# A hybrid RG-LRU and attention layer on one core: scores in one run, the gate row inside w_o, a regrouped last stage

## The chip, the cores and the metric

The kernel runs on one core of one Trainium2 chip. The metric is device time in microseconds (us); three runs of the kernel before have a median of 577.61 us (577.07 to 577.84). Engines: TensorE (PE) multiplies matrices into PSUM, which has eight banks of 128x512 float32; VectorE (DVE), ScalarE (ACT) and GpSimd (POOL) work element by element; SyncE (SP) issues the loads and stores.

## The reference

One encoder layer on x of 512 tokens by 1024 channels, in float32. With h = rms_norm(x) * (1 + scl) + shift (shift, scl and a gate row come from c), one product h @ w_in gives eight parts of 1024 columns: xa, za, q, k, v, zb, ga, gb. Then two branches are merged:

```
xa  = conv4(xa); per direction: r, i = sigmoid(block_diag(xa)); a = exp(-8 r softplus(-lam))
h   = scan of a*h + sqrt(1 - a^2) * (i*xa), forward and backward
y_a = ((h_fwd + h_bwd) * silu(za)) @ w_pa
y_b = (neighbourhood_attention(q, k, v, rpb) * silu(zb)) @ w_pb     # 16 heads of 64, window 8 x 16
merged = sigmoid(ga) * y_a + sigmoid(gb) * y_b
out = rms_norm(x + gate * (merged @ w_o), g_final)
```

The gate is a row of 1024 numbers, one for each column of the output, so it multiplies the product merged @ w_o column by column.

## The kernel before

**Precision and shapes.** Every product of two float32 matrices is done as three TensorE matmuls on a high and a low part (helper mm3, recorded at line 342): high by high, high by low, low by high. The high part is a cast on ScalarE (line 336), the low part a subtraction on VectorE or GpSimd (line 339). Channels lie on the 128 partitions and the 512 tokens along the free axis, so a projection tile of 128 columns of w_in is 8 x 3 = 24 matmuls of 128x512 into one PSUM bank (class acc).

**Stages.** First the norm, h and v; then for each of eight head pairs the projections of q, k and z with the attention of the pair between them; then four groups of two channel tiles of the recurrent branch (projections, gates, scan) with y_b @ w_pb; then ga, y_a @ w_pa and the merge; at the end the output product.

**What sets the order.** The operations are not issued as they are written. Each is given to a planner (class Plan) with an engine, a cost, a rank, and the tiles that it reads and writes; the planner runs a list schedule and fixes one order per engine. It also hands out the slots of SBUF and the eight banks of PSUM. LIMITS says how many banks a class may hold: acc 3, sp (scores) 2, pt (transposes) 2, pv (products with v) 2, mi 2, gt (gates) 4.

**Attention of a pair** (function attention, line 682). The 512 queries are four blocks of 128; two heads lie on partitions 0 to 63 and 64 to 127. half(b0) does two blocks: scores issues 12 matmuls with 64 rows, 192 or 256 columns, into two sp banks (one per head); VectorE adds the bias and takes the minimum (line 718); ScalarE takes the exponential (724); TensorE transposes (733, tile pt); ScalarE and VectorE split the transposed block (738, 740, tile pp); TensorE multiplies with v (tile pv); ScalarE and VectorE add the parts (755, 758, 761, tiles vp and yt). After both halves come the reciprocals (tile rcx, transposed at line 781 into mi) and the product with silu(zb).

**Gates** (conv_gates, line 851). For each channel tile and each direction d, 6 matmuls with 64 rows write two gt banks, which ScalarE reads with four tanh.

**The gate row and w_o.** gate_row (line 968) builds the row, broadcast to 128 partitions, in two halves of 512 columns (tiles gate) with half the value, and g_final likewise (gfin). w_o is loaded in eight blocks of 128 rows (tile wo), cast (woh) and split (wol) from line 1033 on. The output product goes tile by tile of 128 tokens; mhl is the merged tile. Its first 512 columns (o0) are followed by the other 512 (o1), those of the last tile in two pieces of 256.

**The epilogue** (epi, line 1049) for each piece: multiply by gate (1055), add x (1057), squares and their sum on ScalarE (1065; on VectorE, line 1061, for the last piece), multiply by g_final (1067), and once a tile is whole, the root and its refinement (rstd_ops, lines 409 to 418), the scaling, and stores from SyncE (1084, 1087, 1090).

Of the kernel before, what the change touches and what calls it, by code (L numbers as in the profile page):

```python
# [13 lines left out]
P = 128  # L14
S = 512
D = 1024
# [15 lines left out]
LIMITS = {"hx": 8, "acc": 3, "sp": 2, "pt": 2, "pv": 2, "mi": 2, "gt": 4}  # L32
# [261 lines left out]
def layer(ctx, tc, x, par, w_m, w_g, bc_gate, w_v, w_in, w_blk, rpb, amask, w_pa, w_pb, w_o, g_final, out):  # L294
# [387 lines left out]
    def attention(pr, q, k, z, nbt, pos):  # L682
# [10 lines left out]
        off = (pr % 2) * 256  # L693
        def half(b0):
            sp = [B("sp"), B("sp")]
            spv = lambda h, e: sp[h].ap.rearrange("p (e f) -> p e f", e=2)[:, e, :]
            rk = pos + 0.1 * b0
            nks = [ROWS * BLOCKS[b0 + e][1] for e in range(2)]

            def scores(e_):  # L700
                for e in range(2):
                    kc0, w, _ = BLOCKS[b0 + e]
                    for i, (qt, kt) in enumerate(((qh, kh), (qh, kl), (ql, kh))):
                        for h in range(2):
                            kv = kt.ap.rearrange("p (r c) -> p r c", c=GW)[H[h], :, kc0:kc0 + w]
                            mm(spv(h, e)[:, :nks[e]], qt.ap[H[h], (b0 + e) * P:(b0 + e + 1) * P], kv, i == 0, i == 2)
            op("PE", 0.85, scores, rk, r=[qh, ql, kh, kl], w=sp, name=f"qk{pr}")
# [143 lines left out]
    def conv_gates(i, xa):  # L851
# [16 lines left out]
        for d in range(2):  # L868
            bk = [B("gt"), B("gt")]

            def f(e_, d=d, bk=bk):
                for m, (w, xx) in enumerate(((g[0], xh), (g[0], xl), (g[1], xh))):
                    for e in range(2):
                        mm(bk[e].ap, w.ap[H[e], c0 + d * P:c0 + (d + 1) * P], xx.ap[H[e], :], m == 0, m == 2)
# [12 lines left out]
            op("DVE", dve(512), lambda e, u=u: nc.vector.scalar_tensor_tensor(u.ap, u.ap, 1.0, xc.ap, op0=ALU.add, op1=ALU.mult),  # L887
               n + 0.6, r=[xc], rw=[u], lock=True, name="ix")
# [160 lines left out]
    def epi(t, c0, w, o, rank, last):  # L1049
# [5 lines left out]
        op("DVE", dve(w), lambda e: nc.vector.tensor_tensor(y(), o.ap[:, :w], gate[n].ap[:, gs], op=ALU.mult), rank,  # L1055
           r=[o, gate[n]], w=[yo[t]], name="e0")
        op("DVE", dve(w), lambda e: nc.vector.tensor_tensor(y(), y(), xr(), op=ALU.add), rank, r=[xres[t, n]], rw=[yo[t]],  # L1057
           lock=True, name="e1")
# [5 lines left out]
        else:  # L1064
            op("ACT", act(w, 0, True), lambda e: nc.scalar.activation(xr(), y(), AF.Square, accum_out=ssq.ap), rank,  # L1065
               r=[yo[t]], w=[ssq, xres[t, n]])
            op(("DVE", "POOL"), (dve(w), pool_(w)), lambda e: ENGINE[e].tensor_tensor(y(), y(), gfin[n].ap[:, gs], op=ALU.mult),  # L1067
               rank + 0.1, r=[gfin[n]], rw=[yo[t]], lock=True, name="e2")
        if not last:
            if t in ssum:  # L1070
                a = ssum[t]
                op("DVE", 0.16, lambda e: nc.vector.tensor_tensor(a.ap, a.ap, ssq.ap, op=ALU.add), rank + 0.1, r=[ssq], rw=[a])
            else:
                ssum[t] = ssq
            return
        rs, a = C("rs", 1, 6), ssum[t]
        rstd_ops(1, [a, ssq], lambda: (a.ap, ssq.ap), rank, rs)
        if final:
            op("DVE", dve(w), lambda e: nc.vector.scalar_tensor_tensor(y(), y(), rs.ap, gfin[n].ap[:, gs], op0=ALU.mult, op1=ALU.mult),
               rank, r=[rs, gfin[n]], rw=[yo[t]], lock=True)  # L1080
            z = lambda: yo[t].ap[:, 512:c0]
            op("DVE", dve2(w), lambda e: nc.vector.tensor_scalar(z(), z(), rs.ap, None, op0=ALU.mult), rank, r=[rs], rw=[yo[t]],
               lock=True)
            op("SP", 0.45, lambda e: nc.sync.dma_start(out[rows, 512:], yo[t].ap[:, 512:]), rank, r=[yo[t]], size=262144)
            zz = lambda: yo[t].ap[:, :512]
            op("ACT", act(512, 1), lambda e: nc.scalar.activation(zz(), zz(), AF.Copy, scale=rs.ap), rank, r=[rs], rw=[yo[t]])
            op("SP", 0.45, lambda e: nc.sync.dma_start(out[rows, :512], zz()), rank, r=[yo[t]], size=262144)
# [103 lines left out]
```

## Time and profile before

| what | value |
|---|---|
| median of three runs | 577.61 us (577.07 to 577.84) |
| profiled execution: time, span | 577.42 us, 575.70 us |
| mean granted TensorE clock | 0.997 |
| busy: PE, DVE, ACT, POOL | 98%, 70%, 59%, 16% |
| chain that ended last: PE, DVE | 97%, 1% |

A page lists the busy time of each engine, the span in slices, the chain of work that ended last, and groups of instructions by line. The timeline of a view merges equal instructions that follow each other (x4) and puts idle time ahead of them in brackets with what ended it. Ends of matmuls are modelled, and they overlap: a 128x512 matmul has a modelled length of 390 ns. Starts are what counts there. The time of the execution is 1.72 us longer than the span, which goes from its first to its last instruction.

### The profile page before, as it was taken

The numbers are of one execution on the slowest core, as the hardware profiler recorded it, in microseconds if no ns is written. First come the engines' busy times: TensorE is split into PE (matmuls) and PEld (weight loads), VectorE is DVE, ScalarE is ACT, GpSimd is POOL, SyncE is SP. The second block draws the span as 40 slices with busy tenths as digits, with TensorE's granted clock in tenths as the row PEclk, the third lists the DMA queues.
The fourth block names the chain that finished last, engine by engine and source line by source line (L and its number), as shares of the span: only waits on it lengthen the run. The fifth ranks groups of instructions, "written<-read, shape, count | busy, mean of one in ns | idle before, by whom it ended". The sixth has DMA issues, their size and how long they took to land.

```text
span 575.7 us, 7726 instructions
## 1 busy us (share of the span) xinstructions
PE 566.2 (98%) x2829; PEld 465.1 (81%) x2829; DVE 404.4 (70%) x690; ACT 337.1 (59%) x584; POOL 91.7 (16%) x82
## 2 busy tenths in 40 slices
PE   8999999999999999999999999999999999999994
PEld 6888878888888888887887787788788888888884
DVE  5997966776776867786479649739847996465444
ACT  5864536646546557469948875993994333252132
POOL 0004428264273470000000000000000000000010
PEclk9999999999999999999999999999999999999998
DMA  8993987544435321123232123123239813380002
GB/s 286 409 406 93 351 246 219 189 112 147 115 96 175 83 101 48 63 77 125 73 111 92 68 79 129 45 102 109 74 95 326 273 38 109 123 316 1 0 38 110
DMA packets 30814, 81.34 MB, mean 141 GB/s; under 512 B 3264, under 2 KB 6456, under 8 KB 30777
## 3 DMA queue, kind: packets, MB, share of 16 engines
q1 hardware_dynamic: 30777, 80.86, 42.3%
q8 instruction: 22, 0.36, 0.3%
q14 instruction: 15, 0.12, 0.1%
HBM read 74.56 MB, written 6.29 MB: 140 GB/s over the span
## 4 chain that ended last, share of the span: by engine, by line
PE 97%; DVE 1%; ACT 0%; issue 0%; POOL 0%; POOLq 0%; ACTq 0%
PE acc L342 76%; PE hx L342 8%; PE pv L342 3%; PE pt L733 3%; PE sp L342 2%; PE gt L342 2%; PE mi L457 2%; PE hx L386 1%; PE hx L471 1%; PE mi L781 1%; ACT xr L1065 0%; DVE yo L1057 0%; DVE yo L1055 0%; DVE q L412 0%; PE mi L342 0%
## 5 line engine op out<-in xcount | busy, mean ns | idle before, releaser
L342 PE MATMUL acc<-hhl,whi 128*128 128x512 f32 x784 | 247.8, 398 | 0.0
L342 PEld LDWEIGHTS acc<-hhl,whi 128*128 128x128 f32 x784 | 141.6, 188 | 29.1 <-issue 2.9
L342 PE MATMUL acc<-hhl,wlo 128*128 128x512 f32 x392 | 153.2, 391 | 0.0
L342 PEld LDWEIGHTS acc<-hhl,wlo 128*128 128x128 f32 x392 | 73.7, 188 | 15.9
L336 ACT CAST whi<-wraw 128x1024 fp32r<-128x1024 f32 x72 | 74.2, 1046 | 3.4 <-DMA wraw<-in_w_in_dram 2.6
L339 DVE TENSOR_TENSOR wlo<-wraw,whi 128x1024 fp32r<-128x1024 f32 x49 | 59.2, 1220 | 12.0 <-ACT whi L336 11.1
L339 POOL TENSOR_TENSOR wlo<-wraw,whi 128x1024 fp32r<-128x1024 f32 x23 | 55.2, 2404 | 73.0 <-ACT whi L336 59.5
L1067 POOL TENSOR_TENSOR yo<-yo,gfin 128x512 f32<-128x512 f32 x4 | 5.2, 1288 | 344.0 <-ACT xr L1065 344.0
L724 ACT ACTIVATE p<-p,mn 128x192 f32<-128x192 f32 (+1 forms) x64 | 30.4, 477 | 28.8 <-DVE mn L718 28.8
L342 PE MATMUL acc<-woh,mhl 128*128 128x512 f32 (+1 forms) x144 | 40.4, 366 | 0.0
L947 DVE SCALAR_TENSOR_TENSOR gm<-gm,acc 128x512 f32<-128x512 f32 x16 | 11.0, 688 | 41.7 <-PE acc L342 41.7
L662 POOL TENSOR_TENSOR nb<-msk,braw 128x192 f32<-128x192 f32 (+1 forms) x48 | 31.0, 677 | 56.4 <-DMA braw<-in_rpb_dram 56.4
L342 PE MATMUL acc<-yahl,whi 128*128 128x512 f32 x128 | 39.5, 390 | 0.0
L342 PE MATMUL acc<-ybhl,whi 128*128 128x512 f32 x128 | 39.4, 390 | 0.0
L718 DVE CUSTOM_DVE_ANT_0 p<-sp,nb 128x192 f32<-128x192 f32 (+1 forms) x64 | 32.4, 614 | 7.6 <-PE sp L342 7.2
L342 PE MATMUL hx<-vh,hhl 128*128 128x512 f32 x112 | 35.4, 391 | 0.0
L740 DVE TENSOR_TENSOR pp<-pt,pp 96x512 fp32r<-96x512 f32 (+1 forms) x32 | 22.0, 687 | 11.7 <-ACT pp L738 11.7
L342 PEld LDWEIGHTS acc<-woh,mhl 128*128 128x128 f32 x144 | 26.1, 189 | 4.4
L342 PEld LDWEIGHTS acc<-yahl,whi 128*128 128x128 f32 x128 | 24.0, 188 | 5.0
L342 PEld LDWEIGHTS acc<-ybhl,whi 128*128 128x128 f32 x128 | 24.0, 188 | 5.0
L342 PE MATMUL acc<-wol,mhl 128*128 128x512 f32 (+1 forms) x72 | 26.3, 366 | 0.0
L758 DVE TENSOR_TENSOR vp<-pv,vp 64x256 f32<-64x256 f32 x32 | 13.5, 421 | 18.1 <-ACT vp L755 17.6
(183 smaller groups left out, 1004.6 us busy)
## 6 DMA issues: line engine op xcount, KB each, us to landing
wraw<-in_w_in_dram SPq DMA_DIRECT2D x56, 512.0 KB
wc<-in_w_m_dram SPq DMA_DIRECT2D x16, 512.0 KB
vscr<-va SPq DMA_DIRECT2D x8, 512.0 KB
vt<-vscr SPq DMA_DIRECT2D x16, 256.0 KB
wraw<-in_w_pb_dram SPq DMA_DIRECT2D x8, 512.0 KB
wraw<-in_w_pa_dram SPq DMA_DIRECT2D x8, 512.0 KB
wr<-in_w_g_dram SPq DMA_DIRECT2D x16, 256.0 KB
wo<-in_w_o_dram SPq DMA_DIRECT2D x8, 512.0 KB
```

What stands on the lines that cost most here:

```text
L336: return lambda e: nc.scalar.copy(o(), i()) if e == "ACT" else nc.vector.tensor_copy(o(), i())
L339: return lambda e: ENGINE[e].tensor_tensor(o(), a(), b().bitcast(F32), op=ALU.subtract)
L342: nc.tensor.matmul(o, a, b, start=first, stop=last)
L386: op("PE", 0.9, lambda e, n=n, cb=cb: nc.tensor.matmul(cb.ap, onesc.ap[0:1, :], crow.ap[0:1, n * 512:(n + 1) * 512], start=True, stop=True ...
L457: op("PE", 0.3, lambda e: nc.tensor.matmul(wb.ap[:, :P], onesc.ap, onesc.ap, start=True, stop=True), 5000 + j, r=[onesc], w=[wb], until=un ...
L662: nc.gpsimd.tensor_tensor(o, mv, view, op=ALU.subtract)
L718: nc.vector.tensor_tensor_reduce(out=o, in0=v(spv(h, e)[:, :nk]), in1=v(hv(nb)[:, h, :nk]), scale=1.0, scalar=3e38, op0=ALU.add, op1=ALU.m ...
L724: nc.scalar.activation(hv(pt_)[:, h, :nk], hv(pt_)[:, h, :nk], AF.Exp, bias=mn.ap[:, h:h + 1], scale=-1.0, accum_out=sm.ap[:, 2 * b + h:2 ...
L733: nc.tensor.transpose(pv4()[:4 * w, h, j, :], hv(pt_)[:, h, j * 4 * w:(j + 1) * 4 * w], ident.ap)
L740: op("DVE", dve(512), lambda e_, w=w, ppv=ppv, pv4=pv4: nc.vector.tensor_tensor(ppv()[:4 * w, :, :, 1, :], pv4()[:4 * w], ppv()[:4 * w, :, ...
L758: op("DVE", dve(256), lambda e_, h=h: nc.vector.tensor_tensor(v3()[H[h]], p3(pv[h])[H[h], :, 1, :], v3()[H[h]], op=ALU.add), rk - 0.45, r= ...
L947: op("DVE", dve(512), lambda e: nc.vector.scalar_tensor_tensor(t.ap, t.ap, 1.0, o.ap, op0=ALU.add, op1=ALU.mult), n - 1.9, r=[o], rw=[t], ...
```

## The change

Five edits. (1) All four blocks of a pair's scores are one operation of 24 matmuls into four sp banks; the limit of sp goes from 2 to 4. (2) The gate matmuls of both directions are one operation of 12 into four gt banks. (3) Each block of w_o is multiplied by the gate row in place on VectorE, two operations of 128x512 for each of eight blocks, before the cast and the split; the epilogue adds x straight to the bank. (4) The partial sums of squares carry the epsilon along; the root takes the last sum with the rest as a bias, and the refinement takes two operations. (5) In the last tile the multiplication by g_final of the second half is left to the end, where it is one operation of 512 columns with the scaling, and the first half is stored from ScalarE's queue.

```diff
-LIMITS = {"hx": 8, "acc": 3, "sp": 2, "pt": 2, "pv": 2, "mi": 2, "gt": 4}
+LIMITS = {"hx": 8, "acc": 3, "sp": 4, "pt": 2, "pv": 2, "mi": 2, "gt": 4}
...
+        sps = [[B("sp"), B("sp")] for _ in range(2)]
+        nkb = [ROWS * w for _, w, _ in BLOCKS]
+
+        def scores(e_):
+            for b, (kc0, w, _) in enumerate(BLOCKS):
+                for i, (qt, kt) in enumerate(((qh, kh), (qh, kl), (ql, kh))):
+                    for h in range(2):
...
+        op("PE", 1.45, scores, pos, r=[qh, ql, kh, kl], w=sps[0] + sps[1], name=f"qk{pr}")
+
         def half(b0):
-            sp = [B("sp"), B("sp")]
+            sp = sps[b0 // 2]
...
-            op("PE", 0.85, scores, rk, r=[qh, ql, kh, kl], w=sp, name=f"qk{pr}")
...
-            op("PE", 0.75, f, n + 0.5 + 0.1 * d, r=[g[0], g[1], xh, xl], w=bk, name="gates")
...
+        op("PE", 1.55, f, n + 0.5, r=[g[0], g[1], xh, xl], w=bks[0] + bks[1], name="gates")
...
+        for n in range(2):
+            v = lambda n=n, raw=raw: raw.ap[:, n * 512:(n + 1) * 512]
+            op("DVE", dve(512), lambda e, n=n, v=v: nc.vector.tensor_tensor(v(), v(), gate[n].ap, op=ALU.mult), rank,
+               r=[gate[n]], rw=[raw], lock=True, name="wog")
...
-        op("DVE", dve(w), lambda e: nc.vector.tensor_tensor(y(), o.ap[:, :w], gate[n].ap[:, gs], op=ALU.mult), rank,
-           r=[o, gate[n]], w=[yo[t]], name="e0")
-        op("DVE", dve(w), lambda e: nc.vector.tensor_tensor(y(), y(), xr(), op=ALU.add), rank, r=[xres[t, n]], rw=[yo[t]],
-           lock=True, name="e1")
+        op("DVE", dve(w), lambda e: nc.vector.tensor_tensor(y(), o.ap[:, :w], xr(), op=ALU.add), rank,
+           r=[o, xres[t, n]], w=[yo[t]], name="e1")
...
-        rs, a = C("rs", 1, 6), ssum[t]
-        rstd_ops(1, [a, ssq], lambda: (a.ap, ssq.ap), rank, rs)
+        op("ACT", 0.21, lambda e: nc.scalar.activation(sd.ap, ssq.ap, AF.Sqrt, bias=a.ap), rank, r=[ssq, a], w=[sd])
+        op("DVE", 0.17, lambda e: nc.vector.tensor_tensor(v.ap, ssq.ap, a.ap, op=ALU.add), rank, r=[ssq, a], w=[v])
+        op("DVE", 0.17, lambda e: nc.vector.reciprocal(r.ap, sd.ap), rank, r=[sd], w=[r])
+
+        def newton(e):
+            nc.vector.scalar_tensor_tensor(q.ap, r.ap, v.ap, r.ap, op0=ALU.mult, op1=ALU.mult)
+            nc.vector.scalar_tensor_tensor(rs.ap, q.ap, -3.0, r.ap, op0=ALU.add, op1=ALU.mult)
...
-            op("DVE", dve2(w), lambda e: nc.vector.tensor_scalar(z(), z(), rs.ap, None, op0=ALU.mult), rank, r=[rs], rw=[yo[t]],
-               lock=True)
...
-            op("SP", 0.45, lambda e: nc.sync.dma_start(out[rows, :512], zz()), rank, r=[yo[t]], size=262144)
+            op("DVE", dve(512), lambda e: nc.vector.scalar_tensor_tensor(z(), z(), rs.ap, gfin[1].ap, op0=ALU.mult, op1=ALU.mult),
+               rank, r=[rs, gfin[1]], rw=[yo[t]], lock=True)
+            op("SP", 0.45, lambda e: nc.sync.dma_start(out[rows, 512:], z()), rank, r=[yo[t]], size=262144)
+            op("ACT", act(512, 1) + 0.5, lambda e: (nc.scalar.activation(zz(), zz(), AF.Copy, scale=rs.ap),
+               nc.scalar.dma_start(out[rows, :512], zz())), rank, r=[rs], rw=[yo[t]])
```

The planner's lists change with it. On TensorE, the end of the first run of scores of the second pair stood like this before (acc are projections; brackets name the engine that an instruction waits for):

```order
L342 MATMUL sp_1115<-kh_1096,ql_1015 128x256
L342 MATMUL sp_1116<-kh_1096,ql_1015 128x256
L342 MATMUL acc_1082<-hhl_509,whi_820 128x512 x2
L342 MATMUL acc_1082<-hhl_509,wlo_829 128x512
L342 MATMUL acc_1082<-hhl_543,whi_820 128x512 x2
L342 MATMUL acc_1082<-hhl_543,wlo_829 128x512
L342 MATMUL acc_1082<-hhl_586,whi_820 128x512 x2
L342 MATMUL acc_1082<-hhl_586,wlo_829 128x512
L342 MATMUL acc_1151<-hh_247,whi_971 128x512 [waits PE_49]
L342 MATMUL acc_1151<-hl_257,whi_971 128x512
L342 MATMUL acc_1151<-hh_247,wlo_985 128x512 [waits Pool_49]
L342 MATMUL sp_1159<-kh_1096,qh_1001 128x256
```

After it, at the same place, the third and fourth block's scores follow at once:

```order
L342 MATMUL sp_1114<-kl_1100,qh_996 128x256
L342 MATMUL sp_1115<-kl_1100,qh_996 128x256
L342 MATMUL sp_1114<-kh_1094,ql_1003 128x256
L342 MATMUL sp_1115<-kh_1094,ql_1003 128x256
L342 MATMUL sp_1116<-kh_1094,qh_996 128x256 [waits PE_49]
L342 MATMUL sp_1117<-kh_1094,qh_996 128x256 [waits PE_49]
L342 MATMUL sp_1116<-kl_1100,qh_996 128x256
```

The projection matmuls that stood between the two runs now stand behind the one run; the list of each of the eight pairs has this form. On VectorE, where w_o begins (wol are its low parts, gm and mhl the merged tiles), the list was:

```order
L339 TENSOR_TENSOR wlo_4816<-wraw_4733,whi_4798 128x1024
L339 TENSOR_TENSOR mhl_4818<-gm_4615,mhl_4818 128x512
L339 TENSOR_TENSOR wol_4852<-wo_4800,woh_4842 128x1024
L339 TENSOR_TENSOR wol_4867<-wo_4803,woh_4857 128x1024
L339 TENSOR_TENSOR wol_4875<-wo_4808,woh_4865 128x1024
L947 SCALAR_TENSOR_TENSOR gm_4705<-gm_4705,acc_4844 128x512
```

and is:

```order
L339 TENSOR_TENSOR wlo_4816<-wraw_4733,whi_4798 128x1024
L339 TENSOR_TENSOR mhl_4818<-gm_4615,mhl_4818 128x512
L1044 TENSOR_TENSOR wo_4800<-wo_4800,gate_4263 128x512
L1044 TENSOR_TENSOR wo_4800<-wo_4800,gate_4268 128x512
L1044 TENSOR_TENSOR wo_4803<-wo_4803,gate_4263 128x512
L1044 TENSOR_TENSOR wo_4803<-wo_4803,gate_4268 128x512
L1044 TENSOR_TENSOR wo_4808<-wo_4808,gate_4263 128x512
L339 TENSOR_TENSOR wol_4868<-wo_4800,woh_4856 128x1024
L339 TENSOR_TENSOR wol_4876<-wo_4803,woh_4863 128x1024
L1044 TENSOR_TENSOR wo_4808<-wo_4808,gate_4268 128x512
```

The multiplications of w_o (line 1044) stand ahead of the splits and between the evacuations of TensorE's banks. On VectorE, from the last tile's final piece on, the list was:

```order
L1072 TENSOR_TENSOR ssq_5118<-ssq_5118,ssq_5285 128x1
L1055 TENSOR_TENSOR yo_5109<-acc_5253,gate_4268 128x256
L1057 TENSOR_TENSOR yo_5109<-yo_5109,xr_4964 128x256
L1061 ISA xr_4964,ssq_5295<-yo_5109 128x256
L1061 ISA ssq_5295 128x1
L409 SCALAR_TENSOR_TENSOR v_1042_5297<-ssq_5118,ssq_5295 128x1
L418 RECIPROCAL r_1044_5301<-sd_1043_5299 128x1
L412 TENSOR_TENSOR q_1045_5303<-r_1044_5301 128x1
L413 TENSOR_TENSOR q_1045_5303<-q_1045_5303,v_1042_5297 128x1
L414 SCALAR_TENSOR_TENSOR rs_5304<-q_1045_5303,r_1044_5301 128x1
L1079 SCALAR_TENSOR_TENSOR yo_5109<-yo_5109,rs_5304,gfin_4275 128x256
L1082 TENSOR_SCALAR yo_5109<-yo_5109,rs_5304 128x256
```

and is (sd comes from ScalarE in both):

```order
L1080 TENSOR_TENSOR ssp_5301<-ssp_5135,ssq_5292 128x1
L1064 TENSOR_TENSOR yo_5125<-acc_5274,xr_4963 128x256
L1068 ISA xr_4963,ssq_5307<-yo_5125 128x256
L1068 ISA ssq_5307 128x1
L1087 TENSOR_TENSOR v_1047_5309<-ssq_5307,ssp_5301 128x1
L1088 RECIPROCAL r_1049_5313<-sd_1048_5311 128x1
L1091 SCALAR_TENSOR_TENSOR q_1050_5315<-r_1049_5313,v_1047_5309 128x1
L1092 SCALAR_TENSOR_TENSOR rs_1051_5316<-q_1050_5315,r_1049_5313 128x1
L1096 SCALAR_TENSOR_TENSOR yo_5125<-yo_5125,rs_1051_5316,gfin_4275 128x512
```

The multiplication by the gate is gone, the sum v (line 1087) stands beside the root, and the last operation has 512 columns.

## Rows read from the trace of the kernel before

**Rows 1.** Part 1 of the page, busy time, share of the span, instructions of each engine.
```profile
PE 566.2 (98%) x2829; PEld 465.1 (81%) x2829; DVE 404.4 (70%) x690; ACT 337.1 (59%) x584; POOL 91.7 (16%) x82
```

**Rows 2.** The waits of TensorE: engine, line, releaser; total, times, longest (us).
```profile
PE mi L457 <- POOL onesc L360: 1.5, 1, 1.5
```

**Rows 3.** Timeline of TensorE, one head pair: start, length (us), operation, tiles, shapes, count.
```profile
147.38 0.39 PE L342 MATMUL acc<-hhl,wlo 128*128 128x512 f32 x1
...
147.89 0.27 PE L342 MATMUL sp<-kl,qh 64*128 64x192 f32 x2
...
148.38 0.29 PE L342 MATMUL sp<-kh,ql 64*128 64x256 f32 x2
...
149.18 0.40 PE L342 MATMUL acc<-hhl,wlo 128*128 128x512 f32 x1
...
151.26 0.39 PE L342 MATMUL acc<-hh,wlo 128*128 128x512 f32 x1
...
151.81 0.29 PE L342 MATMUL sp<-kl,qh 64*128 64x256 f32 x2
...
152.25 0.27 PE L342 MATMUL sp<-kh,ql 64*128 64x192 f32 x2
...
153.39 0.39 PE L342 MATMUL acc<-hhl,wlo 128*128 128x512 f32 x1
```

**Rows 4.** Chain of waits, attention and gates: start, length (us), engine, tile, line, instructions.
```profile
177.26 0.44 PE pt L733 x4
...
233.42 6.12 PE acc L342 x27
...
258.91 1.59 PE gt L342 x12
```

**Rows 5.** Timeline of VectorE, then of TensorE, second half of one pair.
```profile
184.39 0.43 DVE L761 TENSOR_TENSOR yt<-pv,vp 64x256 f32<-64x256 f32 x1
...
185.37 0.63 PE L342 MATMUL pv<-pp,vt 128*128 128x256 f32 x4
```

**Rows 6.** VectorE: one group of part 5's kind, then the timeline around w_o.
```profile
L1018 DVE TENSOR_TENSOR gm<-gm,gm 128x512 f32<-128x512 f32 x8 | 5.5, 691 | 0.3
...
526.11 0.69 DVE L339 TENSOR_TENSOR mhl<-gm,mhl 128x512 fp32r<-128x512 f32 x1 [0.74 <-ACT mhl L336]
538.92 0.69 DVE L1055 TENSOR_TENSOR yo<-acc,gate 128x512 f32<-128x512 f32 x1 [12.12 <-PE acc L342]
```

**Rows 7.** Chain of waits from the end of the last tile but one.
```profile
559.96 2.05 PE acc L342 x9
...
562.04 0.70 DVE yo L1055
```

**Rows 8.** Timeline of all engines, the last tile; idle time and releaser in brackets.
```profile
567.47 0.28 PE L342 MATMUL acc<-woh,mhl 128*128 128x256 f32 x1
...
568.12 0.42 DVE L1055 TENSOR_TENSOR yo<-acc,gate 128x256 f32<-128x256 f32 x1
568.57 0.42 DVE L1057 TENSOR_TENSOR yo<-yo,xr 128x256 f32<-128x256 f32 x1
...
570.12 0.16 DVE L412 TENSOR_TENSOR q<-r 128x1 f32<-128x1 f32 x1
...
570.71 0.48 DVE L1079 SCALAR_TENSOR_TENSOR yo<-yo,rs,gfin 128x256 f32<-128x256 f32 x1
570.77 0.72 ACT L1086 ACTIVATE yo<-yo,rs 128x512 f32<-128x512 f32 x1 [0.87 <-DVE rs L414]
...
571.48 0.33 SPq L1084 DMA_DIRECT2D out_dram<-yo  x1
571.91 0.38 SPq L1087 DMA_DIRECT2D out_dram<-yo  x1
```

**Rows 9.** Busy time, the last stores; last columns: granted TensorE clock, DMA share, GB/s.
```profile
571.90:574.50 2.60, 0.00 (x0) 0.00 (x0) 0.00 (x0) 0.00 (x0) 0.00 (x0) 0.53 0.53 202
```

More of the change, by code (lines that the diff above doesn't have):

```diff
@@ L693, in attention @@
         off = (pr % 2) * 256
+        sps = [[B("sp"), B("sp")] for _ in range(2)]
[4 more added lines that the diff above has]
+                    for h in range(2):
+                        kv = kt.ap.rearrange("p (r c) -> p r c", c=GW)[H[h], :, kc0:kc0 + w]
+                        o = sps[b // 2][h].ap.rearrange("p (e f) -> p e f", e=2)[:, b % 2, :nkb[b]]
+                        mm(o, qt.ap[H[h], b * P:(b + 1) * P], kv, i == 0, i == 2)
+        op("PE", 1.45, scores, pos, r=[qh, ql, kh, kl], w=sps[0] + sps[1], name=f"qk{pr}")
         def half(b0):
-            sp = [B("sp"), B("sp")]
+            sp = sps[b0 // 2]
             spv = lambda h, e: sp[h].ap.rearrange("p (e f) -> p e f", e=2)[:, e, :]
             rk = pos + 0.1 * b0
[L698 to L706, printed above, removed]
-            op("PE", 0.85, scores, rk, r=[qh, ql, kh, kl], w=sp, name=f"qk{pr}")
+            nks = nkb[b0:b0 + 2]
             pv = [B("pv"), B("pv")]
@@ L867, in conv_gates, with f @@
         ri = [T("ri") for _ in range(4)]
-        for d in range(2):
-            bk = [B("gt"), B("gt")]
-            def f(e_, d=d, bk=bk):
+        bks = [[B("gt"), B("gt")] for _ in range(2)]
+        def f(e_):
+            for d in range(2):
                 for m, (w, xx) in enumerate(((g[0], xh), (g[0], xl), (g[1], xh))):
                     for e in range(2):
-                        mm(bk[e].ap, w.ap[H[e], c0 + d * P:c0 + (d + 1) * P], xx.ap[H[e], :], m == 0, m == 2)
-            op("PE", 0.75, f, n + 0.5 + 0.1 * d, r=[g[0], g[1], xh, xl], w=bk, name="gates")
+                        mm(bks[d][e].ap, w.ap[H[e], c0 + d * P:c0 + (d + 1) * P], xx.ap[H[e], :], m == 0, m == 2)
+        op("PE", 1.55, f, n + 0.5, r=[g[0], g[1], xh, xl], w=bks[0] + bks[1], name="gates")
+        for d in range(2):
+            bk = bks[d]
             c = 16 * d + i
@@ L1066, in epi @@
                r=[yo[t]], w=[ssq, xres[t, n]])
-            op(("DVE", "POOL"), (dve(w), pool_(w)), lambda e: ENGINE[e].tensor_tensor(y(), y(), gfin[n].ap[:, gs], op=ALU.mult),
-               rank + 0.1, r=[gfin[n]], rw=[yo[t]], lock=True, name="e2")
+            if t < NT - 1 or n == 0:
+                op(("DVE", "POOL"), (dve(w), pool_(w)), lambda e: ENGINE[e].tensor_tensor(y(), y(), gfin[n].ap[:, gs], op=ALU.mult),
+                   rank + 0.1, r=[gfin[n]], rw=[yo[t]], lock=True, name="e2")
@@ L1069, in epi @@
         if not last:
[L1070 to L1074, printed above, removed]
-            return
-        rs, a = C("rs", 1, 6), ssum[t]
-        rstd_ops(1, [a, ssq], lambda: (a.ap, ssq.ap), rank, rs)
-        if final:
-            op("DVE", dve(w), lambda e: nc.vector.scalar_tensor_tensor(y(), y(), rs.ap, gfin[n].ap[:, gs], op0=ALU.mult, op1=ALU.mult),
-               rank, r=[rs, gfin[n]], rw=[yo[t]], lock=True)
-            z = lambda: yo[t].ap[:, 512:c0]
-            op("DVE", dve2(w), lambda e: nc.vector.tensor_scalar(z(), z(), rs.ap, None, op0=ALU.mult), rank, r=[rs], rw=[yo[t]],
-               lock=True)
-            op("SP", 0.45, lambda e: nc.sync.dma_start(out[rows, 512:], yo[t].ap[:, 512:]), rank, r=[yo[t]], size=262144)
-            zz = lambda: yo[t].ap[:, :512]
-            op("ACT", act(512, 1), lambda e: nc.scalar.activation(zz(), zz(), AF.Copy, scale=rs.ap), rank, r=[rs], rw=[yo[t]])
-            op("SP", 0.45, lambda e: nc.sync.dma_start(out[rows, :512], zz()), rank, r=[yo[t]], size=262144)
@@ new lines, in epi @@
+            a = ssum.get(t)
+            ssum[t] = b = C("ssp", 1, 10)
+            op("DVE", 0.16, (lambda e: nc.vector.tensor_tensor(b.ap, a.ap, ssq.ap, op=ALU.add)) if a else
+               (lambda e: nc.vector.tensor_scalar(b.ap, ssq.ap, D * EPS, None, op0=ALU.add)), rank, r=[ssq] + [a] * bool(a), w=[b])
+            return
+        a = ssum[t]
+        v, sd, r, q, rs = (C(f"{g}1", 1) for g in ("v", "sd", "r", "q", "rs"))
+        op("ACT", 0.21, lambda e: nc.scalar.activation(sd.ap, ssq.ap, AF.Sqrt, bias=a.ap), rank, r=[ssq, a], w=[sd])
```

2 lines of the change are left out of this document (added).

## The prediction

> **What bounds the kernel now.** I read the busy totals first: TensorE is busy for 98% of the span [rows 1]. A busy TensorE can still be a waiting one, so the waits of TensorE come next. There is one in the whole run, 1.5 us at the start, for a constant that GpSimd writes [rows 2]; from there to the last tile the matrix engine never waits for data, a bank or a transfer. So before the tail only an edit that makes TensorE's own list shorter can gain time, and an edit that lengthens VectorE's list costs nothing until TensorE has to wait. The chain of waits then shows where that ends: at 562.01 us the chain leaves TensorE, and the last 13.7 us are a relay of VectorE, ScalarE and the two last stores [rows 7, 8]. Every shortened step on that relay counts in full, up to the point where another one is later. These are the two places the sum is made of.
>
> **The scores.** Before, a head pair issues two runs of 12 small matmuls with 12 projection matmuls between them; now it issues one run of 24. The same 24 matmuls are streamed, so what can go is what a run costs beyond its columns: the wait on entry and the slow start and end. I measure a run by the starts of the projection matmuls round it. Undisturbed, projection matmuls follow each other every 0.227 us (27 in 6.12 us) [rows 4]. So, by the starts in [rows 3]:
> - First run: from the start at 147.38 to that at 149.18 are 1.80 us, which hold three projection matmuls (0.68). The run costs 1.12.
> - Second run with the transposes behind it: 151.26 to 153.39, 2.13 less 0.68, is 1.45. Four transposes alone take 0.44 [rows 4], so the second run costs 1.01.
> - Inside a run, a group (two heads, 12 matmuls make six groups) follows the one before it after 0.11 us (151.81 to 152.25, four steps) to 0.12 us (147.89 to 148.38, four steps).
> In the merged run the second half is six more groups at that pace: 0.66 to 0.74, I take 0.70 as the middle of the two rows. So a pair costs 1.12 + 0.70 = 1.82 where it cost 2.13, and 0.31 us go. The order of TensorE has the same picture in all eight pairs: 8 times 0.31 is 2.5 us, of which I take 2.4. Upper bound: the faster pace (0.35 a pair) and another 0.03 for whatever the neighbours of the lost run gain, 3.0 in all. Lower bound below nothing: the third and fourth bank are entered in the middle of the run behind a wait of their own; if that costs as much as a new entry, nothing is saved, and the transposes no longer start straight from a run of scores, which made the second run 0.11 cheaper than the first; that would be a loss of 8 times 0.11, 0.9 us. I stay at the upper side, since nothing between the halves changes the shape of the matmuls.
>
> **The gates.** Both directions of a tile already stand in one piece: 12 matmuls, 1.59 us [rows 4], and the list of TensorE before has eight such pieces, none of 6. The new operation asks for four banks at once, which were four banks before too. I cost this edit at nothing on either side.
>
> **What the scores ask of the others.** All four banks of scores are held together, and the minima of the third and fourth block come earlier on VectorE. The tightest place that I find is the third product with v, which needs its two banks back from the last addition of the first half: that addition starts at 184.39 and takes 0.43, and the product starts at 185.37, so 0.55 us are to spare [rows 5]. In the new order that product again stands 12 projection matmuls and one group of transposes behind the fourth block's transposes. On VectorE the subtraction for q moves ahead of the additions, one operation of about 0.7; but the projection that it reads now ends before the fourth block's transposes and no longer behind them, three projection matmuls (0.68) sooner. So the margin stays near half a microsecond, and I count nothing.
>
> **The gate row in w_o.** VectorE gets 16 more operations of 128x512 with two operands in SBUF, 0.691 each as the same form has elsewhere [rows 6]: 11.1 us, in front of the splits of w_o and among the evacuations. ScalarE's casts of w_o wait for them. What hides them: the last operand of the output product is the split of the last merged tile, done at 526.80; the first evacuation of that product starts at 538.92, and TensorE uses the operand in the three matmuls (0.68) ahead of it; VectorE idled for 12.12 us between the two [rows 6]. Even if no earlier gap took a share, the last split would end at 526.80 + 11.06 = 537.86, ahead of the 538.2 at which TensorE wants it. Cost: nothing; without that cover it would be the 11.1 us. Ahead of an evacuation that frees one of TensorE's banks stand at most three of these operations in a row, 2.1 us, while the next bank is wanted a whole projection (24 matmuls, 5.4 us) later. SyncE's list keeps the same loads in the same order; only its last store leaves it.
>
> **The tail.** Counting from TensorE's last matmul, which starts at 567.47 and is modelled 0.28 long, so it ends at 567.75 [rows 8]. One tile earlier VectorE started 0.03 after TensorE's end (562.01 to 562.04) [rows 7]; I take 567.79 for the last tile.
> - Before, it began only at 568.12, since the chain from 562.04 on VectorE and ScalarE was late [rows 7, 8]. That chain loses one operation of 0.70 [rows 7] and would reach the last tile by 567.42; so now TensorE is the later one. Gain 0.33.
> - Multiplying by the gate and adding x become one operation: 568.12 to 568.57, gain 0.45.
> - The sum before the square root is no longer on the path (the root takes it as a bias): one operation on one column. The refinement has two such operations and not three. Each takes (570.71 - 570.12) / 3 = 0.197 [rows 8], so 0.39.
> - Two halves of 256 (570.71 to 571.48, 0.77) become one operation of 512, 0.69 by [rows 6] and 0.03 to the store: gain 0.05.
> Together 1.22 us, to the issue of the first store, which moves from 571.48 to 570.26. ScalarE's half (0.72, begun 0.06 behind VectorE's) [rows 8] is ready at about 570.3 and goes out on its own queue.
> What does the second queue add? Before, the stores were issued 0.43 apart (571.48, 571.91). In the 2.6 us from 571.90 on, the DMA engines are busy for a share of 0.53 with them [rows 9], 1.38 us. One store is half of that, 0.69, more than 0.43, so the second store was already waiting for them, and issuing it earlier moves nothing: the end follows the first issue, by 1.38 us of transfers and what lies ahead of and behind them. By the other reading, that the end follows the last issue, 571.91 to 570.3, the tail would gain 1.6. The Trainium skill ("DMA: Bandwidth & Descriptors", section "Issuing engines are not separate DMA queues") says that transfers from several issuers run on the same 16 engines and that only issue time is saved; that speaks for the first reading and against a gain from the second queue by itself. I take 1.2; ends 0.8 (a store from ScalarE, which issued none before, is issued later than SyncE does it, by as much as SyncE's spacing of 0.43) and 1.6.
>
> **The sum.** The profiled execution took 577.42 us, its span 575.70. 577.42 - 2.4 - 1.2 = 573.8. The median of the three runs, 577.61, lies 0.19 above the profiled one; I name 573.9.
>
> **Rivals.**
> - *The merge gives nothing* (a new entry at the third bank): the tail alone, 577.42 - 1.2 = 576.2, with the loss bound above 577.1. For it: a wait for TensorE's own earlier work stands at the third and fourth bank. Against it: such a wait stands at the second run's second bank before too, and the run there costs no more. Chance 0.08, most of it within 0.2%.
> - *The tail gives nothing*: the store from ScalarE's queue, whose first use it is, is late by as much as the chain gained: 577.42 - 2.4 = 575.0. Nothing in the trace shows that queue. Chance 0.08, still faster.
> - *TensorE starts to wait for banks* in the attention: of eight banks four hold scores, and the third product with v waits for its banks. It decides once VectorE's additions come 0.55 us later than I count [rows 5]; each us beyond costs 8 us, one per pair. To come out slower by 0.2% TensorE must lose 3.6 + 1.2 = 4.8 us, 0.6 a pair, so additions late by 1.15. If a stray 1.5 us operation falls ahead of them, it is 8 times 0.95: 573.8 + 7.6 = 581.4. Against it: the addition shows its plain length [rows 5], and nothing but TensorE's own results and one ScalarE copy stands before it. The Trainium skill warns of this in "TensorEngine Tiling (Array Packing)", section "Gotcha 1: PSUM Pressure": matmuls on row tiles need more banks; no wait in the trace of before shows it here. Chance 0.06.
>
> **How the numbers follow.** The forecast, 2.4 and 1.2 with their bounds, has 0.78; its own range is 572.8 (3.0 and 1.6) to 575.2 (1.4, with two fifths of the scores' gain lost, and 0.8). The range for 8 in 10 is 572.6 to 575.6, which takes in a lost tail and leaves out the rest. What a measurement of this kernel can tell from no change is about 0.2%, 1.2 us: faster means below 576.4. Faster: 0.78, the lost tail 0.08 and a part of the first rival, 0.89. Within: 0.06. Slower: 0.05.
>
> **What would show it.** Right: one run of 24 score matmuls per pair, 1.55 to 1.65 us from its first start to the next projection matmul; still a single wait of TensorE; its last matmul starting near 565.1; VectorE's last tile starting within 0.1 of TensorE's end; the two stores issued within 0.2 of each other and then transfers of 1.4 us in one piece. Wrong: any wait of TensorE with a product with v, or an operand of the output product, as its place; VectorE still working on the gate row when TensorE wants the last split; a store from ScalarE's queue that starts over 0.5 us behind the other.

## The result, and the profile after

The changed kernel takes 573.71 us (median of four runs, 573.27 to 574.08) against 577.69 for the kernel before, run beside it: a ratio of 0.9933, 95% interval 0.9916 to 0.9950, or 3.9 us less by the ratio. The forecast was 573.9. Its profiled execution took 573.27 us, span 571.4 (before 577.42 and 575.7). One execution of the last experiment ran at a granted clock of 0.851 and took 628.42 us, all others of the study at 0.993 or more; it is left out below.

I cut every trace into four stretches of time, called legs: to the start of the first score matmul; from there to the start of TensorE's last matmul ("body"); from there to the issue of the first of the two last stores ("tail"); from there to the end of the span.

| us | first score | body | tail | behind |
|---|---|---|---|---|
| before | 79.37 | 488.10 | 4.01 | 4.22 |
| after | 79.18 | 485.34 | 2.97 | 3.93 |
| less | 0.19 | 2.76 | 1.05 | 0.30 |

The first leg is not the change's: in the fourteen profiled executions of this study it lies between 78.40 and 80.33 with no relation to the edits. The body repeats to 0.01 us where TensorE's list is the same and no operand comes late: 488.10 in two kernels, 486.58 in two, 485.34 in three. So bodies and tails tell apart what the times can't. (Legs are differences of times of one profiled execution per kernel, good to 0.01 us.)

The totals of the page (PEld are TensorE's weight loads):

```profile
PE 563.2 (99%) x2829; PEld 464.6 (81%) x2829; DVE 393.1 (69%) x693; ACT 336.6 (59%) x584; POOL 99.1 (17%) x84
```

TensorE does the same 2829 matmuls in 3.0 us less busy time [rows 1], and its waits are still the one row of [rows 2]. The timeline of TensorE for one head pair (start, duration, shapes), in place of [rows 3]:

```profile
146.16 0.39 PE L342 MATMUL acc<-hhl,wlo 128*128 128x512 f32 x1
146.48 0.36 PE L342 MATMUL sp<-kh,qh 64*128 64x192 f32 x2
...
147.16 0.29 PE L342 MATMUL sp<-kh,ql 64*128 64x256 f32 x2
147.29 0.28 PE L342 MATMUL sp<-kh,qh 64*128 64x256 f32 x2
...
148.05 0.73 PE L342 MATMUL acc<-hhl,whi 128*128 128x512 f32 x2
148.62 0.40 PE L342 MATMUL acc<-hhl,wlo 128*128 128x512 f32 x1
```

From 146.16 to 148.62 are 2.46 us, less three projection matmuls (0.68) 1.78: the forecast had 1.82. The third bank, entered at 147.29, comes 0.13 after the group before it, an ordinary step; no new entry is paid there. The tail, timeline of all engines, in place of [rows 8]:

```profile
564.52 0.28 PE L342 MATMUL acc<-woh,mhl 128*128 128x256 f32 x1
564.83 0.42 DVE L1064 TENSOR_TENSOR yo<-acc,xr 128x256 f32<-128x256 f32 x1 [0.86 <-PE acc L342]
...
565.76 0.29 ACT L1086 ACTIVATE sd<-ssq,ssp 128x1 f32<-128x1 f32 x1 [1.98 <-DVE ssq L1068]
...
566.28 0.22 DVE L1091 SCALAR_TENSOR_TENSOR q<-r,v 128x1 f32<-128x1 f32 x1
...
566.73 0.75 DVE L1096 SCALAR_TENSOR_TENSOR yo<-yo,rs,gfin 128x512 f32<-128x512 f32 x1
...
567.48 0.40 ACTq L1100 DMA_DIRECT2D out_dram<-yo  x1
567.51 0.33 SPq L1098 DMA_DIRECT2D out_dram<-yo  x1
```

VectorE now waits for TensorE (0.86) and starts 0.03 behind its end; the two stores leave 0.03 apart. The root (sd) takes 0.29; in the kernel before it took 0.20:

```profile
569.69 0.20 ACT L417 ACTIVATE sd<-v 128x1 f32<-128x1 f32 x1 [2.01 <-DVE v L409]
```

Behind the stores, in windows (the last two columns are the DMA engines' share and GB/s):

```profile
568.00:568.50 0.50, 0.00 (x0) 0.00 (x0) 0.00 (x0) 0.00 (x0) 0.00 (x0) 0.50 0.27 102
568.50:569.00 0.50, 0.00 (x0) 0.00 (x0) 0.00 (x0) 0.00 (x0) 0.00 (x0) 0.50 1.01 389
569.00:569.50 0.50, 0.00 (x0) 0.00 (x0) 0.00 (x0) 0.00 (x0) 0.00 (x0) 0.50 1.02 389
569.50:570.00 0.50, 0.00 (x0) 0.00 (x0) 0.00 (x0) 0.00 (x0) 0.00 (x0) 0.50 0.47 168
```

0.5 times the shares is 1.39 us of transfers in one piece, as before [rows 9].

### The profile page after: what moved, and what is told of

Read it like the earlier page. It is cut to its first block, busy times and chain, and to the rows that moved or that the text cites. A ratio compares the mean times of both kernels' runs of the same rounds, so it can differ in the third digit from the quotient of the medians.

```text
span 571.4 us, 7735 instructions
## 1 busy us (share of the span) xinstructions
PE 563.2 (99%) x2829; PEld 464.6 (81%) x2829; DVE 393.1 (69%) x693; ACT 336.6 (59%) x584; POOL 99.1 (17%) x84
## 4 chain that ended last, share of the span: by engine, by line
PE 96%; DVE 2%; ACT 1%; issue 0%; POOL 0%; POOLq 0%; DVEq 0%; ACTq 0%
PE acc L342 77%; PE hx L342 7%; PE pv L342 3%; PE pt L736 2%; PE gt L342 2%; PE sp L342 2%; PE hx L386 1%; PE mi L784 1%; PE mi L457 1%; DVE wc L501 0%; PE hx L471 0%; ACT x L446 0%; DVE junk L436 0%; ACT xT L336 0%; ACT vh L336 0%
## 5 line engine op out<-in xcount | busy, mean ns | idle before, releaser
L1075 POOL TENSOR_TENSOR yo<-yo,gfin 128x512 f32<-128x512 f32 x6 | 8.1, 1352 | 338.4 <-ACT xr L1072 338.3
L662 POOL TENSOR_TENSOR nb<-msk,braw 128x192 f32<-128x192 f32 (+1 forms) x48 | 34.6, 756 | 55.4 <-DMA braw<-in_rpb_dram 55.4
L721 DVE CUSTOM_DVE_ANT_0 p<-sp,nb 128x192 f32<-128x192 f32 (+1 forms) x64 | 31.1, 615 | 16.7 <-PE sp L342 16.7
L342 PE MATMUL acc<-yahl,wlo 128*128 128x512 f32 x64 | 24.9, 389 | 0.0
```

The lines of the kernel that those rows point to most:

```text
L342: nc.tensor.matmul(o, a, b, start=first, stop=last)
L662: nc.gpsimd.tensor_tensor(o, mv, view, op=ALU.subtract)
L721: nc.vector.tensor_tensor_reduce(out=o, in0=v(spv(h, e)[:, :nk]), in1=v(hv(nb)[:, h, :nk]), scale=1.0, scalar=3e38, op0=ALU.add, op1=ALU.m ...
```

## The experiments

All medians, with the ratio to the kernel before on the same chip and its 95% interval; legs are those of the profiled execution.

**The scores alone** (`e1_scores`). The merged score operation in the kernel before, nothing else (code is cut and abridged here and below):

```
-LIMITS "sp": 2
+LIMITS "sp": 4
-op("PE", 0.85, scores, rk, ..., w=sp)                  # twice, 12 matmuls
+op("PE", 1.45, scores, pos, ..., w=sps[0] + sps[1])    # once, 24
```

> The kernel before with the scores of four blocks in one run of 24 into four banks, and nothing else of the change. Theory: each separate run of score matmuls costs about 0.35 us beside its own columns (0.35 us less from pair to pair in the changed kernel), so the eight removed runs give 8 x 0.35 = 2.8 us, 574.8 us, with TensorE still waiting once only. Rival A (the run costs nothing, the whole gain lies in the epilogue): 577.6 us. Rival B (the four banks held longer give part of it back, and the other edits of the change had freed it): TensorE waits for banks reappear in the trace, and the time lies between 575.5 and 577.6 us.

576.80 us, 0.9979 [0.9970, 0.9987]: 1.1 less, where 2.8 was expected. The body is 486.58, 1.52 below before and 1.24 above the changed kernel, with no wait of TensorE added. So neither rival fits. The time shows less than the legs, because the part outside the span is longer: 2.1 to 2.2 us in all eleven executions, against 1.6 to 1.7 in those of the kernel before; why is not known. The chain of waits in one stretch of the recurrent half (start, length), first of the changed kernel, then of this one:

```profile
304.45 1.59 PE gt L342 x12
306.04 9.06 PE acc L342 x39
315.11 1.58 PE gt L342 x9
```

```profile
307.83 1.59 PE gt L342 x12
309.42 3.62 PE acc L342 x15
313.04 0.89 PE gt L342 x5
313.93 2.26 PE acc L342 x9
316.19 0.90 PE gt L342 x6
```

(The chain counts 9 and 5 where TensorE's timeline has 12 and 6.) The second run of gates has fallen apart into two of 6 with nine projection matmuls between them, and TensorE's list has three such places. The list of before had none. Where the two directions are two operations, the planner is free to place projection matmuls between them; why it does so in this list and not in the old one was not tried.

**The tail alone** (`e2_tail`), edits 3 to 5 in the kernel before:

```
+wo block *= gate row (16 x)            # ahead of the splits
-y = acc * gate; y = y + x
+y = acc + x
-v = ssq0 + ssq1; sd = sqrt(v)
+sd = sqrt(ssq1, bias=ssp)
-store half 0 and half 1 from SyncE
+store half 0 from ScalarE, half 1 from SyncE
```

> The kernel before with the gate row in w_o, the other order of the normalisation at the end and the two store queues, scores and gates as before. Theory: the stretch from the last matmul to the first store falls from 4.01 to 2.96 us as in the changed kernel, so 576.5 us, and 576.2 us if the 0.3 us that the changed kernel also saves behind its first store belongs to these edits. Rival (the tail is worth nothing by itself): 577.6 us. With the scores alone the two gains should add up to the whole, 3.9 us, within 0.5 us.

576.61 us, 0.9982 [0.9973, 0.9991]. Body 488.10 as before, tail 2.97, behind it 3.74. The tail's gain is its own, as the theory says; with the scores alone (1.2 and 1.0 by the ratios) it does not add up to 3.9. Part of that is again the time outside the span, 1.8 to 2.1 us here. By the legs 1.52 and 1.05 are there, of 3.81 for body and tail together; the 1.24 that is missing comes two experiments below.

**The gates alone** (`e3_gates`):

```
-op("PE", 0.75, gates of direction d, w=bk)             # twice, 6 matmuls
+op("PE", 1.55, gates of both, w=bks[0] + bks[1])       # once, 12
```

> The kernel before with the gate matmuls of two directions in one run of 12, and nothing else. Theory: the run already stood in one piece in the list before (12 together, 1.59 us in both traces), so 577.6 us, within 0.3 us. Rival (an entry saved for each of the eight pairs of gate runs, as with the scores): 574.8 us.

577.84 us, 0.9997 [0.9988, 1.0006], body 488.10: nothing, as expected.

**The change without the gates** (`e10_no_gates`), the reverse of the edit above in the changed kernel:

> The changed kernel with the gates of the two directions issued as two operations of six again, all other edits kept. In its list three of the eight gate runs of 12 fall apart into 6, nine projection matmuls, 6, as they do in the kernel with the scores alone; in the kernel before none does. Theory: a split costs about as much as a separate score run, (310.48 - 309.25) / 3 = 0.41 us from the first gate matmul to the last matmul of the two traces, so 573.7 + 1.2 = 574.9 us, and the scores alone, the tail alone and this then add up to the whole. Rival (what the scores alone lacked lies elsewhere, in the start of the program or the order behind it): 573.7 us within 0.3 us.

575.11 us, 0.9959 [0.9946, 0.9971]; body 486.58, that of the scores alone to the hundredth, with the same three splits; tail 2.97. So the gate edit is worth 1.24 us in the changed kernel and nothing in the kernel before: it doesn't make a run shorter, it keeps the planner from cutting it. The legs now add up, 1.52 + 1.05 + 1.24 = 3.81. The two lists also place some projection matmuls differently, which was not tried apart; 1.24 over three splits is 0.41, what one score run more costs below.

**Four banks, two operations** (`e7b_two_ops`): the changed kernel with the two score operations of before and the limit of four.

```
-op("PE", 1.45, scores, pos, ..., w=sps[0] + sps[1])
+op("PE", 0.85, scores, rk, ..., w=sp)                  # twice
```

> The changed kernel with the scores as two operations of 12 with two banks each, as before, but with four banks allowed: the list then puts the two runs side by side by itself, 24 in one run, and the transposes of two blocks side by side too (8 in one run), one run of transposes fewer per pair. Theory (the neighbourhood of the matmuls counts, not the operation that holds them; transposes have no price of their own run): 573.7 us within 0.4 us. Rival A (the runs of transposes cost as much as those of scores): 573.7 - 2.8 = 570.9 us. Rival B (the earlier merge needs all four banks claimed at once): 576.5 us.

573.22 us, 0.9929 [0.9916, 0.9941]; body 484.68. Theory right: the neighbourhood counts. The body is 0.66 shorter than the changed kernel's, some 0.08 a pair. Transposes stand eight in a row in seven of the eight pairs, but products with v and projection matmuls are placed differently too, and which of it gives the 0.66 is not shown. This is the fastest kernel of the study, by less than the times can tell.

**Two runs, three runs** (`e5a_two_runs`, `e5b_three_runs`): the changed kernel with the scores as one operation a block, held behind chosen groups of the third projection.

```
-op("PE", 1.45, scores, pos, ...)
+for b in range(4):   # blocks released by groups 4,4,6,6 (three runs: 4,4,6,7)
+    op("PE", 0.45, scores of b, pos, ..., after=[group])
```

> The changed kernel with the scores in two runs of 12 with six projection matmuls between them, four banks allowed and everything else kept; its list is otherwise that of the kernel with two operations. Theory (each separate run costs 0.35 us): 8 x 0.35 = 2.8 us more, 576.5 us. Rival (it was the number of banks or the later wait for them, not the number of runs): 573.7 us.

576.31 us, 0.9978 [0.9969, 0.9987]; body 488.05, 3.37 above the list with one run (`e7b_two_ops`, the same but for the last pair): 0.42 for each of eight runs more. Theory right, with a somewhat higher price.

> The same with three runs of 12, 6 and 6 (four of 6 in the first pair). Theory: 8 x 0.35 = 2.8 us more than with two runs, and 0.35 us for the fourth run of the first pair, 579.6 us, on a line with one and two runs. Rival A (a run of 6 matmuls pays less at its edges, or only the first cut costs): 577 us or less. Rival B (the runs are so late that the softmax behind them makes TensorE wait): new waits of TensorE in the pairs, over 580 us.

578.54 us, 1.0024 [1.0014, 1.0034]; body 490.75, another 2.70. TensorE's timeline has three runs (12, 6, 6) in every pair, the first too, so these are eight runs more, not nine, at 0.34 each. That is the theory's price, for a run of 6 as well; no wait of TensorE in the pairs, so not rival B. The runs that this kernel adds have transposes straight behind them, as the second run of the kernel before had, where the pair lost 0.34 too (22.77 to 22.43 us from one pair's first score to the next). The runs of `e5a_two_runs` have projections on both sides and cost 0.42. Where a run's price lies is seen by its edges. First the weight loads of the changed kernel (timeline of PEld, the ones round a run):

```profile
145.94 0.19 PEld L342 LDWEIGHTS acc<-hhl,wlo 128*128 128x128 f32 x1
146.48 0.18 PEld L342 LDWEIGHTS sp<-kh,qh 64*128 64x128 f32 x2 [0.35 <-issue]
...
148.05 0.30 PEld L342 LDWEIGHTS acc<-hhl,whi 128*128 128x128 f32 x2
```

Among projection matmuls a load starts 0.22 ahead of its matmul (145.94 and 146.16). At the first score it starts with the matmul, 146.48, after 0.35 of idling, and again at the first projection matmul behind the run, 148.05. The load that runs ahead of its matmul elsewhere stands bare at both edges. Whether the bare load is the cause or only goes along with it is not shown. The two-run kernel shows what the edges cost, around its first run and ahead of its second:

```profile
149.31 0.29 PE L342 MATMUL sp<-kh,ql 64*128 64x256 f32 x2
149.53 0.74 PE L342 MATMUL acc<-hhl,whi 128*128 128x512 f32 x2
150.11 0.40 PE L342 MATMUL acc<-hhl,wlo 128*128 128x512 f32 x1
...
150.81 0.39 PE L342 MATMUL acc<-hhl,wlo 128*128 128x512 f32 x1
151.13 0.39 PE L342 MATMUL sp<-kh,qh 64*128 64x256 f32 x2
151.35 0.28 PE L342 MATMUL sp<-kl,qh 64*128 64x256 f32 x2
```

Behind a run the step to the projection is 0.22 where steps inside a run are 0.11, and the two matmuls from 149.53 take 0.58 where two take 0.45; ahead of a run the last projection matmul takes 0.32 (150.81 to 151.13) and not 0.23. That is 0.33 a run, and 0.44 with the first step inside it (0.22 from 151.13, where later ones are 0.11). Runs of matmuls of full height (128 rows) have no such edges. Four transposes between projections in the changed kernel:

```profile
151.38 0.39 PE L342 MATMUL acc<-hhl,wlo 128*128 128x512 f32 x1
151.61 0.60 PE L736 MATMUL pt<-ident,p 128*96 128x128 f32 x4
151.96 0.71 PE L342 MATMUL acc<-hhl,whi 128*128 128x512 f32 x2
152.51 0.40 PE L342 MATMUL acc<-hhl,wlo 128*128 128x512 f32 x1
```

From 151.38 to 152.51 are 1.13, less three projection matmuls (0.68) 0.45: four steps of 0.11 and nothing more. Yet the load at 151.94 behind them is almost bare too, 0.02 ahead of its matmul.

**One queue** (`e4_one_queue`): the changed kernel, its first half stored by SyncE again.

```
-ScalarE: scale half 0, then dma_start(half 0)
+ScalarE: scale half 0;  SyncE: dma_start(half 0)
```

> The changed kernel with both stores of the last tile issued by SyncE again, everything else kept. Reading one (the end follows the first issue, and the transfers run in one piece of 1.4 us): 573.7 us, within 0.2 us. Reading two (the second queue is what saves the 0.3 us that the changed kernel is shorter behind its first store): the stretch from the first store to the end is 4.2 us again instead of 3.9 us, 574.0 us. Reading three (the second store stands behind the first on its queue for its whole issue, 0.4 us): 574.1 us or more, with a gap between the two transfers in the windows.

573.81 us, 0.9939 [0.9925, 0.9953]. The stores leave 0.46 apart and their transfers still run in one piece (timeline of SyncE's queue, then windows):

```profile
567.81 0.33 SPq L1098 DMA_DIRECT2D out_dram<-yo  x1
568.27 0.35 SPq L1100 DMA_DIRECT2D out_dram<-yo  x1
```

```profile
568.50:569.00 0.50, 0.00 (x0) 0.00 (x0) 0.00 (x0) 0.00 (x0) 0.00 (x0) 0.69 0.72 266
569.00:569.50 0.50, 0.00 (x0) 0.00 (x0) 0.00 (x0) 0.00 (x0) 0.00 (x0) 0.50 0.97 369
569.50:570.00 0.50, 0.00 (x0) 0.00 (x0) 0.00 (x0) 0.00 (x0) 0.00 (x0) 0.50 1.03 385
570.00:570.50 0.50, 0.00 (x0) 0.00 (x0) 0.00 (x0) 0.00 (x0) 0.00 (x0) 0.50 0.14 45
```

The stretch behind the first store is 4.06. Over all traces it is 4.06 to 4.23 with one queue (four) and 3.74 to 4.19 with two (ten; means 4.14 and 3.94). So the second queue may be worth some 0.2 us, less than its spread and half of the issue time it saves; the times do not separate readings one and two. The Trainium skill ("DMA: Bandwidth & Descriptors", section "Issuing engines are not separate DMA queues") lets a second issuer save issue time only; 0.2 of 0.46 agrees with that.

**More work on w_o** (`e6a_more8`, `e6b_more16`): identity operations beside the multiplication by the gate row.

```
+if k < 4:   # 8 for the second kernel
+    wo block = max(wo block, wo block)   # VectorE, 128x512, two halves per k
```

> The changed kernel with 8 more VectorE operations of 128x512 in the preparation of w_o (each takes the maximum of a block with itself, so that nothing changes in value). 8 x 0.69 = 5.5 us more on VectorE. Theory (the 16 multiplications by the gate row cost nothing because the stage has some 5.2 us of room behind the last split, at 530.1 us with the first use at 535.3, and 2.8 us of gaps before it): 573.7 us within 0.3 us. Rival (the cover is already used up by the 16): up to 5.5 us more, 579 us.

573.68 us, 0.9941 [0.9928, 0.9955]; body 485.59, 0.25 above the changed kernel's, with the same list of TensorE and no wait more in the list of waits. Theory right by the time, but not in the room it counts: the last split now ends at 536.19, and TensorE takes it at 536.25, 0.35 behind the matmul before instead of 0.23; the next step is 0.11 longer too. That is the 0.25: the cover is just used up, and the gaps of 2.8 gave nothing.

> The same with 16 more, 16 x 0.69 = 11.1 us. Theory: the room of 5.2 us and the gaps of 2.8 us are exceeded by 11.1 - 8.0 = 3.1 us, TensorE waits in the last stage for a split of w_o, 576.8 us. Rival (the rest of the stage gives way and the cover is larger): 573.7 us and no wait.

579.60 us, 1.0044 [1.0032, 1.0057]; body 491.16, 5.82 more. The cover ends, as expected, but the price is nearly twice the 3.1 of the theory. TensorE's waits (total, times, longest), and the last split on VectorE's timeline, here and in the changed kernel:

```profile
PE acc L342 <- DVE wol L339: 1.9, 3, 0.8
...
PE acc L342 <- ACT mhl L336: 0.9, 1, 0.9
PE acc L342 <- ACT woh L336: 0.7, 2, 0.3
```

```profile
540.91 0.69 DVE L339 TENSOR_TENSOR mhl<-gm,mhl 128x512 fp32r<-128x512 f32 x1
```

```profile
529.40 0.69 DVE L339 TENSOR_TENSOR mhl<-gm,mhl 128x512 fp32r<-128x512 f32 x1
```

The last split moves from 529.40 to 540.91; less the later start (79.60 - 79.18 = 0.42) these are 11.1 us, all 16 operations. The gaps ahead of it, 2.8, absorbed nothing, and 11.1 less the room of 5.2 is 5.9, which is the loss. The waits add up to only 3.5 of it, because the profile counts a wait from the modelled end of the matmul before, 0.39 us behind its start, where the next one ordinarily starts after 0.23:

```profile
531.48 0.39 PE L342 MATMUL acc<-woh,mhl 128*128 128x512 f32 x1
532.21 0.49 PE L342 MATMUL acc<-woh,mhl 128*128 128x512 f32 x1 [0.34 <-ACT woh L336]
```

By the starts this wait costs 0.50 (0.73 less 0.23), not 0.34. Counted so, the steps into the six waits and into two that the list leaves out, with four longer steps straight behind them, hold 5.7 of the 5.8; elsewhere the pace is that of the changed kernel.

**The gate row behind w_o** (`e9_gate_in_epilogue`):

```
-wo block *= gate row (16 x)
-y = acc + x
+y = acc * gate; y = y + x
```

> The changed kernel with the gate row multiplied behind w_o again, as an operation of its own before the residual is added; the other order of the normalisation and the two queues are kept. Theory: in the last piece one operation of 256 columns more stands between the last matmul and the store, 0.45 us with its gap, and VectorE comes late to the last piece by 0.33 us again, as in the kernel before: 573.7 + 0.45 to 0.8 = 574.2 to 574.5 us. Rival (the gain of the tail lies in the end of the normalisation alone): 573.7 us.

573.62 us, 0.9938 [0.9925, 0.9950]: by the time alone the rival. The legs tell more: body 485.34, tail 3.43, 0.46 longer, and the first leg ended at 78.40, the earliest of all. The timeline:

```profile
563.74 0.28 PE L342 MATMUL acc<-woh,mhl 128*128 128x256 f32 x1
564.06 0.42 DVE L1060 TENSOR_TENSOR yo<-acc,gate 128x256 f32<-128x256 f32 x1
564.52 0.42 DVE L1062 TENSOR_TENSOR yo<-yo,xr 128x256 f32<-128x256 f32 x1
```

The operation costs its 0.46 on the path, but VectorE starts on time, 0.04 behind TensorE's end: with the other edits in place the gate row does not make it late. In the kernel before, what stood straight ahead of the last piece was another operation, the multiplication by g_final, which waited for ScalarE's squares and ran until the last piece began:

```profile
567.71 0.43 DVE L1067 TENSOR_TENSOR yo<-yo,gfin 128x256 f32<-128x256 f32 x1 [0.88 <-ACT xr L1065]
```

Edit 5 takes it away from there. Whether taking out the gate row alone would have done as well was not tried. By the ratios this kernel is 0.3 us longer than the changed one (0.9938 against 0.9933), which the intervals do not tell from nothing.

**A smaller last piece** (`e8b_384_128`), on the kernel with two score operations:

```
-w = 256 if t == NT - 1 else 512                                  # at h * 256
+w, hc = ((384, 0), (128, 384))[h] if t == NT - 1 else (512, 0)   # at hc
```

> The kernel with two score operations and four banks (573.2 us), with the second half of the last tile in pieces of 384 and 128 columns instead of 256 and 256. What stands behind the last matmul gets shorter, an addition and a square of 256 columns, 0.42 us each, to 128 columns, about 0.13 us each. Theory A (24 matmuls of 128 columns take half of the 0.12 us of those with 256): 573.2 - 0.26 = 573.0 us. Theory B (they take 0.11 us, as the transposes of 128 columns do, 0.44 us for four): 24 x 0.05 = 1.2 us later at the last matmul, 574.2 us. I hold B for likelier.

574.13 us (four executions), 0.9946 [0.9933, 0.9960]. Theory B: the tail is 2.70, 0.27 shorter, and the body 1.08 longer. The matmuls of 128 columns follow each other after 0.11 us (23 steps in 2.52, up to the last one below) and those of 384 after 0.17, together 0.28 where two of 256 take 0.24:

```profile
565.79 0.28 PE L342 MATMUL acc<-wol,mhl 128*128 128x128 f32 x1
565.91 0.28 PE L342 MATMUL acc<-woh,mhl 128*128 128x128 f32 x1
```

## Why the prediction was right, point by point

- *The scores, 2.4.* Right in mechanism, a little small: the body lost 2.76 (0.34 from pair to pair). A separate run costs 0.34 to 0.42 us by the runs added, the lower price where transposes stand behind it, as behind the run that went. The pair's own count, 1.78 for the merged run, was 0.04 under the forecast of 1.82.
- *The gates, nothing on either side.* This step failed, though the sum did not. It rested on the old list, in which the gates stand whole. In the list that the scores make they don't, and the gate edit is worth 1.24 us there. The scores' 2.4 needed it: by themselves they give 1.5. That the total came out is luck in this term, since the same change without the gate edit takes 575.11.
- *Banks and the third product with v.* Right: no new wait of TensorE in the attention in any kernel with the merged scores.
- *The gate row in w_o, nothing.* Right in the result, with some 5 us to spare: 5.5 us more cost 0.25, 11.1 us more cost 5.8. But the worst case of the working was not as safe as it says. It set the last split, 537.86, against TensorE at 538.2 in the kernel before; less the forecast's own 2.4 that is 535.8 (535.5 measured), so TensorE would have waited some 2 us. What saved it are earlier gaps of VectorE, which the worst case had left out: the last split ended at 530.09, only 3.3 later than before.
- *The tail, 1.22.* Measured 1.05, the four terms one by one: VectorE no longer late 0.34 (0.33 forecast, for the lost gate operation; with that operation put back it was not late either); multiplication and addition merged 0.45 (0.45; 0.46 when undone); one-column operations 0.24 (0.39); last operation 0.02 (0.05). The third term is the mis-sized one: two operations of 0.197 did go, but the root with a bias from memory takes 0.29 (565.76) where it took 0.20, and the first merged refinement step 0.22 where plain ones take 0.16.
- *The second queue, nothing by itself.* Not refuted; at most some 0.2 us.
- *The rivals.* A merge that gives nothing, a tail that gives nothing, and waits for banks each failed on its own row: the third bank at 147.29, the stores at 567.48 and 567.51, the waits of TensorE.

2.76 + 1.05 are 3.81 of the 3.9 us. The 0.30 behind the stores and the 0.19 of the first leg are smaller than what these legs differ by between the profiled executions of this study (0.5 and 1.9 us).

## What to carry to other kernels

On an engine that never waits, count the places where matmuls of another tile size begin and end, and not only their columns: here every run of 64-row matmuls among those of 128 rows cost 0.34 to 0.42 us, and runs of 128-row transposes nothing. Where a planner sets the order, an edit is priced against the list that the other edits make: compare the two lists for every kind of run, also the kinds an edit doesn't touch. And when time differs by less than the spread, cut the traces at fixed events: a leg that repeats to 0.01 us shows what a median of runs can't.

## What the hardware showed that I had not expected

- The price of a run of half-height matmuls (64 rows) sits at its two edges, where the weight loads start with their matmul and not 0.22 us ahead of it. The Trainium skill ("TensorE: Matmul & The Clock Gate", section "The mechanism") says that a load is pulled ahead of running matmuls when its row group does not conflict with theirs or when it goes to the background weight buffer. The trace agrees in so far as full-height loads behind full-height matmuls run ahead; why those at a change of height do not, no run here shows.
- Full-height transposes have no such price: four of them between projections take 0.45 us, four steps of 0.11.
- Matmuls of 128 columns follow each other after 0.11 us, those of 256 after 0.12.
- The square root of one column takes 0.29 us with a bias from memory and 0.20 without.
- Late splits cost TensorE more than the waits that the profile lists: 5.8 us for waits of 3.5, and 0.25 for none at all.
